# One output piece of a Fourier mixer in other tiles, and a new order of the kernel's front

## The chip, the cores and the metric

The kernel runs on one core of one Trainium2 chip. The metric is the time of one execution on the device in microseconds (us). Several executions were timed; their median is given, and one more was recorded by the hardware profiler.

## The reference

Two layers act on x, a sequence of 512 tokens of width 1024, under a conditioning vector c. Each has a token mixer and then a SwiGLU feed-forward network of width 2816. The mixer of layer 0 is a Fourier mixer, that of layer 1 a retention of 4 heads.

```python
c_act = jax.nn.silu(c)
...
mod = c_act @ w_ada[i] + b_ada[i]
sh1, sc1, g1, sh2, sc2, g2 = jnp.split(mod, 6, axis=-1)
h = modulate(rmsnorm(x, norm_mix_g[i]), sh1, sc1)
...
f = jnp.fft.fftn(hg, axes=(1, 3), norm="ortho").real.astype(h.dtype)
return f.reshape(B, S, D) @ w_o
...
x = x + g1[:, None, :] * m
h = modulate(rmsnorm(x, norm_ffn_g[i]), sh2, sc2)
x = x + g2[:, None, :] * swiglu(h, w_ffn_in[i], w_ffn_out[i])
```

`hg` is h in 4 groups of 256 channels, `w_o` is w_fourier_out. `modulate(h, shift, scale)` is `h * (1 + scale) + shift`; the six vectors of `mod` are named here (0,0) to (0,5) for layer 0: shift, scale and gate of the mixer, then shift (0,3), scale (0,4) and gate (0,5) of the feed-forward network.

## The kernel before, in words

**Products.** Every float32 matrix product is made of three products of rounded parts: high·high, high·low, low·high (`mm3`, L210 to L212). A weight piece of 128x1024 comes by DMA from the SP queue into a buffer `raw` (a pool of 8, so that a load waits until a buffer's last reader is done); `split` makes its high part on ACT (a cast, L204) and its low part on DVE (raw minus high, L205). The parts go into pools `highs` and `lows` of 5 buffers each, or, where the dict `homes` names a step, into two of the 14 held tiles `a0` to `a13` that are idle then (`high_low`, L310 to L324). For the four pieces of w_fourier_out that make the second half of the output channels, `by_dma` takes another way: ACT writes low = -raw (L319), GpSimd (POOL) starts an accumulating DMA that adds the piece from HBM (L321), and ACT casts the high part (L322).

**Conditioning.** A row block of w_ada is multiplied by c_act on DVE and summed (`conditioning`, L399, 128x1024); 8 such pieces, 0 to 7, make one vector of `mod`, and L411 and L414 close it with bias and gain. `settle(key, q)` runs the steps up to piece q.

**The front** (`front`, L654 to L792). It loads x in 4 row blocks, the sequence table in two pieces (into a12 and a13) and w_ada pieces. `squares`, `operand` and `table` make the rounded parts; `sums(m, n)` are the 12 sequence-transform products of block m for half n of the channels; `turn(m)` transposes block m of x on PE and copies it on ACT; `scaled(g)` writes channel group g, scaled by (0,1), to a tile (ACT, L737); `sines_of(g)` makes sine products (L744). In here `InOrder` fixes the order of ACT's and of PE's instructions as written.

**The Fourier output.** `sums_of_two(g)` and `lows_of_two(g)` make the cosine products of group g (L801), combine them with the sines on DVE (L808, L809), and make the two parts (cast L812, low L815). `out_product` then multiplies by w_fourier_out for the first 512 channels, and `out_product_last` for the others, in 256-token halves. Each result is added to x with gate (0,2) by `add_gated` (DVE, L579); its squares are summed over transposes of x on PE (L434); when a half's squares are complete, 1/rms is spread over partitions by two transposes (L459). Then the normed x is modulated (DVE L482, ACT L486 and L487), its low parts are made, and blocks are added and subtracted for a Strassen-like scheme (L516).

**The first feed-forward units** (`first_unit`). Unit 0 is plain (`PlainUnit`, L934), and unit 1 follows with `following.ps("12")` (L888). The pieces of their weights are here called by the buffer numbers of their parts: high/low 1142/1143, 1148/1149, 1154/1155 and 1160/1161 belong to unit 0, 1166/1167 and 1217/1218 to unit 1.

Outside `InOrder` the framework's scheduler sets each engine's order when the program is built. DVE, ACT, POOL and SP then work through their lists as they stand.

Of the kernel before, what the change touches and what calls it, by code (L numbers as in the profile page):

```python
# [156 lines left out]
def trunk(ctx, tc, A, where, out):  # L157
# [16 lines left out]
    def ps():  # L174
        return psum.tile([P, 512], F32, name="ps")
# [7 lines left out]
    def held(tag, dtype=F32R):  # L183

        return hpool.tile([P, D], dtype, name=tag)

    def tok(m):
        return slice(m * P, (m + 1) * P)

    def half(n):  # L190
        return slice(n * 512, (n + 1) * 512)
# [4 lines left out]
    def k2(t):  # L196
        return t.rearrange("p (k c) -> p k c", k=2)
# [453 lines left out]
    def fourier():  # L651
# [3 lines left out]
        def front():  # L655
# [26 lines left out]
            ch = [both[:, 3 * p * P : 3 * (p + 1) * P] for p in range(2)]  # L682
            issue(12)

            def turn(m):
                for k in range(2):
                    o = ps()
                    for j in range(4):
                        nc.tensor.transpose(o[:, tok(j)], xin[m][:, tok(4 * k + j)], ident)
                    for i in range(2):  # L690
                        src, dst = k2(o[:, part(i)]), k2(x[2 * k + i])
                        if m < 2:
                            nc.scalar.copy(out=dst[:, :, tok(m)], in_=src)
                        elif m == 2:
                            nc.scalar.copy(out=dst[:, :, hs : hs + 1], in_=src[:, :, 0:1])
                            nc.scalar.copy(out=dst[:, :, S - P + 1 : S], in_=src[:, :, P - 1 : 0 : -1])
                        else:
                            nc.scalar.copy(out=dst[:, :, hs + 1 : hs + 1 + P], in_=src[:, :, ::-1])
# [3 lines left out]
            def table(p):  # L702
                tabs.append((held(f"a{2 * p}"), held(f"a{2 * p + 1}")))
                split(*tabs[p], tab[p])
# [26 lines left out]
                    nc.tensor.matmul(banks[d], v[:, tok(d)], t[:, c], start=m == k == 0, stop=m == 3 and k == 2)  # L731

            def scaled(g):
                t = k2(held(f"a{g}", F32))
                for k in range(2):
                    d = 2 * g + k
                    nc.scalar.mul(out=t[:, k, :], in_=banks[d], mul=mods[0, 1][:, d : d + 1])  # L737
                a.append(t)
# [14 lines left out]
            with InOrder(tc, mybir.EngineType.Activation, mybir.EngineType.PE):  # L753
                nc.vector.tensor_scalar(out=gains, in0=gains, scalar1=1.0 / RS, scalar2=None, op0=ALU.mult)
                scales = bias[:, 0 : len(SCALES) * ND]
                nc.vector.tensor_scalar(out=scales, in0=scales, scalar1=1.0, scalar2=None, op0=ALU.add)
                squares(0)
                table(0)
                operand(0)
                sums(0, 0)  # L760
                squares(2)
                for n, c in enumerate(cs):
                    nc.scalar.activation(out=c_act[:, half(n)], in_=c, func=AF.Silu)
                squares(1)
                operand(2)
                settle((0, 1), 0)
                table(1)
                operand(1)
                turn(0)
                sums(2, 0)  # L770
                squares(3)
                operand(3)
                settle((0, 1), 3)
                turn(2)
                sums(1, 0)
                turn(1)
                sums(3, 0)
                settle((0, 1), 7)
                sums(0, 1)
                scaled(0)  # L780
                scaled(1)
                sums(2, 1)
                sines_of(0)
                sums(1, 1)
                settle((0, 0), 1)
                turn(3)
                sums(3, 1)
                scaled(2)
                scaled(3)
                sines_of(2)  # L790
            made.update(ch=ch, a=a, sines=sines)

        def halves_of(g):

# [48 lines left out]
        add(lambda: ordered(front))  # L843
        names = [[("wo", n, g) for g in range(4)] for n in range(2)]
        by_dma.update(names[1])
        for g in range(2):
            add(lambda g=g: ordered(lows_of_two, g))
            add(lambda g=g: ordered(sums_of_two, g))
        add(lambda: ordered(lows_of_two, 2))

        def between(g):
# [90 lines left out]
    def first_unit(u, following, channels=False):  # L942


        spread = lambda t, k: add(lambda: made["norm"].spread(t, k))
        if channels:
            homes[*u.key, "00", 0] = 4, 11
            add(last_sums)
            u.p(0, 0, 0)
            spread(0, 1)  # L950
            u.p(0, 0, 1)
            add(lambda: made["norm"].rate(1))
            spread(1, 0)
            u.p(0, 1, 0)
            spread(1, 1)
            u.p(0, 1, 1)
        else:
            homes[*u.key, "00", 0] = 3, 10
            homes[*u.key, "01", 0] = 5, 12
            u.p(0, 0, 0)  # L960
            add(last_sums)
            u.p(0, 0, 1)
            u.p(0, 1, 0)
            add(lambda: made["norm"].scale(1))
            u.p(0, 1, 1)
        following.ps("12")
        for k in range(2):
            for n in range(2):
                u.p(1, k, n)
# [379 lines left out]
```

## Time and profile before

| | |
|---|---|
| median of 3 executions | 1231.36 us (1231.19 to 1231.99) |
| profiled execution | 1231.14 us |
| its span in the trace | 1229.3 us |
| TensorE (PE) busy | 1203.0 us, 98% |
| VectorE (DVE) busy | 1042.1 us, 85% |
| ScalarE (ACT) busy | 583.5 us, 47% |
| GpSimd (POOL) busy | 4.5 us |
| mean granted clock of TensorE | 0.996 |

Busy is the time in which an engine had an instruction of its own in work. The sum over the span does not tell which engine sets the time of a stage; that is read from the stage's waits. The execution's time is 1.84 us more than its span.

### The profile page before, as it was taken

What the parts mean: (1) busy time and instruction counts of PE and PEld (TensorE: products, weight loads), DVE (VectorE), ACT (ScalarE), POOL (GpSimd) and SP (SyncE); (2) the same over time, 40 slices, a digit from 0 to 9 for tenths busy, and PEclk for the clock granted to TensorE, in tenths of its full rate; (3) what the DMA queues carried; (4) which work ended last, traced back from release to release, by engine and by line L of the source; (5) the groups of instructions that cost most, each with busy time, mean ns of one, the idle gap of its engine ahead of it and who ended that gap; (6) DMA issues with size and microseconds to landing.
All of it is one profiled execution on the core that took longest, in us unless ns stands there. A gap on an engine that the chain in (4) does not pass through costs nothing.

```text
span 1229.3 us, 20956 instructions
## 1 busy us (share of the span) xinstructions
PE 1203.0 (98%) x8456; PEld 1129.0 (92%) x8456; DVE 1042.1 (85%) x1702; ACT 583.5 (47%) x890; POOL 4.5 (0%) x12
## 2 busy tenths in 40 slices
PE   7999999999999999999999999999999999999996
PEld 6789998999999899999999999889999898989986
DVE  7989999889899669999898999956997787878755
ACT  5617653434345356455453554522765243434524
POOL 0000000000000000000000000000000000000000
PEclk9999999999999999999999999999999999999998
DMA  9994257464636522224243247852035243434302
GB/s 364 342 330 178 87 184 261 165 213 140 220 120 213 198 104 67 73 87 131 74 141 110 73 150 245 312 182 84 18 120 187 91 153 120 156 119 155 120 1 69
DMA packets 59872, 189.26 MB, mean 154 GB/s; under 512 B 6016, under 2 KB 14336, under 8 KB 59776
## 3 DMA queue, kind: packets, MB, share of 16 engines
q1 hardware_dynamic: 59200, 185.83, 44.3%
q0 software_dynamic: 576, 2.10, 0.9%
q8 instruction: 66, 1.08, 0.4%
q14 instruction: 30, 0.25, 0.1%
HBM read 180.57 MB, written 7.34 MB: 153 GB/s over the span
## 4 chain that ended last, share of the span: by engine, by line
PE 83%; DVE 8%; ACT 4%; DMA 2%; issue 2%; POOL 0%; SPq 0%; ACTq 0%; POOLq 0%; DVEq 0%
PE ps L888 46%; PE ps L211 11%; PE ps L210 11%; PE ps L212 11%; DVE low L205 2%; PE ps L934 2%; DVE raw L347 1%; PE ps L731 1%; ACT t4k L487 1%; PE ps L434 1%; DMA high<-in_w_ada 1%; DMA t4k<-in_x 1%; DMA low<-in_w_fourier_out 1%; ACT a L486 1%; ACT high L204 1%
## 5 line engine op out<-in xcount | busy, mean ns | idle before, releaser
L204 ACT CAST high<-raw 128x1024 fp32r<-128x1024 f32 x255 | 266.2, 1050 | 272.1 <-PE ps L888 80.0
L888 PE MATMUL ps<-a,high 128*128 128x256 f32 x2736 | 365.5, 283 | 2.2 <-ACT a L204 1.3
L205 DVE TENSOR_TENSOR low<-raw,high 128x1024 fp32r<-128x1024 f32 x255 | 310.4, 1221 | 64.0 <-ACT high L204 62.9
L888 PEld LDWEIGHTS ps<-a,high 128*128 128x128 f32 x2736 | 345.7, 192 | 4.7 <-ACT a L204 1.5
L888 PE MATMUL ps<-a,low 128*128 128x256 f32 x1368 | 192.1, 283 | 0.0
L210 PE MATMUL ps<-t4k,high 128*128 128x512 f32 (+1 forms) x512 | 182.2, 356 | 0.0
L211 PE MATMUL ps<-t4k,high 128*128 128x512 f32 (+1 forms) x512 | 179.0, 350 | 0.0
L212 PE MATMUL ps<-t4k,low 128*128 128x512 f32 (+1 forms) x512 | 178.7, 349 | 0.0
L888 PEld LDWEIGHTS ps<-a,low 128*128 128x128 f32 x1368 | 176.4, 192 | 0.1
L399 DVE SCALAR_TENSOR_TENSOR raw<-raw,c_act 128x1024 f32<-128x1024 f32 x97 | 117.7, 1221 | 26.6 <-DMA raw<-in_w_ada 17.3
L212 PEld LDWEIGHTS ps<-t4k,low 128*128 128x128 f32 x512 | 96.6, 189 | 12.6
L888 PE MATMUL ps<-high,a 128*128 128x256 f32 x784 | 107.0, 283 | 1.0 <-ACT t2k L897 0.7
L579 DVE SCALAR_TENSOR_TENSOR x<-ps,mod,x 128x512 f32<-128x512 f32 (+1 forms) x132 | 81.0, 634 | 31.6 <-PE ps L212 31.3
L210 PEld LDWEIGHTS ps<-t4k,high 128*128 128x128 f32 x512 | 96.7, 189 | 11.9
L211 PEld LDWEIGHTS ps<-t4k,high 128*128 128x128 f32 x512 | 96.9, 189 | 11.7
L897 ACT COPY t2k<-ps 128x512 f32<-128x512 f32 x96 | 56.2, 586 | 98.0 <-PE ps L888 95.2
L888 PEld LDWEIGHTS ps<-high,a 128*128 128x128 f32 x784 | 100.4, 192 | 2.5 <-ACT t2k L897 0.9
L901 DVE TENSOR_TENSOR t2k<-t2k,ps 128x512 f32<-128x512 f32 x96 | 65.5, 683 | 13.7 <-ACT t2k L897 8.7
L347 DVE TENSOR_TENSOR raw<-raw 128x1024 f32<-128x1024 f32 x62 | 75.6, 1219 | 0.2
L212 PE MATMUL ps<-a,low 128*128 128x512 f32 (+1 forms) x160 | 56.2, 352 | 2.8 <-DMA low<-in_w_fourier_out 2.8
L204 ACT CAST t4k<-t2k 128x512 fp32r<-128x512 f32 x73 | 45.0, 619 | 29.1 <-DVE t2k L1007 20.8
L210 PE MATMUL ps<-a,high 128*128 128x512 f32 (+1 forms) x160 | 56.9, 359 | 0.2 <-ACT t2k L807 0.2
(157 smaller groups left out, 1428.7 us busy)
## 6 DMA issues: line engine op xcount, KB each, us to landing
raw<-in_w_ffn_in SPq DMA_DIRECT2D x86, 512.0 KB, 4.1
raw<-in_w_ada SPq DMA_DIRECT2D x81, 512.0 KB, 4.5
raw<-in_w_ret_in SPq DMA_DIRECT2D x48, 512.0 KB, 3.3
raw<-in_w_ffn_out SPq DMA_DIRECT2D x44, 512.0 KB, 3.9
raw<-in_w_ret_out SPq DMA_DIRECT2D x16, 512.0 KB, 4.9
raw<-in_w_ada_final SPq DMA_DIRECT2D x16, 512.0 KB, 3.5
raw<-in_w_fourier_out SPq DMA_DIRECT2D x8, 512.0 KB, 7.9
t4k<-in_w_ada SPq DMA_DIRECT2D x7, 512.0 KB, 9.5
```

What stands on the lines that cost most here:

```text
L204: nc.scalar.copy(out=dst_h, in_=src)
L205: nc.vector.tensor_tensor(out=dst_l, in0=src, in1=f32(dst_h), op=ALU.subtract)
L210: nc.tensor.matmul(o, ah, bh, start=first, stop=False, **kw)
L211: nc.tensor.matmul(o, ah, bl, start=False, stop=False, **kw)
L212: nc.tensor.matmul(o, al, bh, start=False, stop=last, **kw)
L347: eng.tensor_tensor(out=dst, in0=p, in1=q, op=ALU.subtract)
L399: nc.vector.scalar_tensor_tensor(out=t, in0=t, scalar=1.0, in1=c_act, op0=ALU.mult, op1=ALU.mult, accum_out=v[:, q : q + 1])
L579: nc.vector.scalar_tensor_tensor(out=xt(j)[:, sl], in0=o, scalar=mods[key][:, j : j + 1], in1=xt(j)[:, sl], op0=ALU.mult, op1=ALU.add)
L888: nc.tensor.matmul(o[:, j * 256 : (j + 1) * 256], a, b, start=tag in "127" and n == m == j == k == 0, stop=n == 1 and k == 3, skip_group_c ...
L897: nc.scalar.copy(out=t, in_=o)
L901: nc.vector.tensor_tensor(out=t, in0=t, in1=self.z if tag == "5" else o, op=ALU.add)
L934: nc.tensor.matmul(o[:, j * 256 : (j + 1) * 256], a, b, start=k == n == m == j == c == 0, stop=k == n == 1 and c == 3, skip_group_check=True,)
```

## The change

Four things are done. (1) The last piece of w_fourier_out, ("wo", 1, 3), gets the held tiles a4 and a11 for its parts; the first piece of the first feed-forward unit, which had these, goes to the pools. (2) `scaled(g)` writes to a12, a13, a2 and a3, where the raw and the split tables were, and no longer to a0 to a3. (3) `turn` is split into `turn` (PE) and `keep` (ACT), and the front is written in another order: SiLU of c first, x turned sooner. (4) `sines_of(2)` stands behind `sums_of_two(0)`, so cosine products of group 0 come first.

```diff
-            def turn(m):
-                for k in range(2):
-                    o = ps()
+            turned = {}
+            def turn(m):
+                turned[m] = [ps() for _ in range(2)]
+                for k, o in enumerate(turned[m]):
                     for j in range(4):
                         nc.tensor.transpose(o[:, tok(j)], xin[m][:, tok(4 * k + j)], ident)
+            def keep(m):
+                for k, o in enumerate(turned.pop(m)):
                     for i in range(2):
...
-                t = k2(held(f"a{g}", F32))
+                t = k2(held(f"a{(12, 13, 2, 3)[g]}", F32))
...
+                for n, c in enumerate(cs):
+                    nc.scalar.activation(out=c_act[:, half(n)], in_=c, func=AF.Silu)
+                cs.clear()
                 squares(0)
+                turn(0)
                 table(0)
                 operand(0)
                 sums(0, 0)
                 squares(2)
-                for n, c in enumerate(cs):
-                    nc.scalar.activation(out=c_act[:, half(n)], in_=c, func=AF.Silu)
                 squares(1)
+                turn(2)
                 operand(2)
-                settle((0, 1), 0)
                 table(1)
                 operand(1)
-                turn(0)
+                squares(3)
+                keep(0)
                 sums(2, 0)
-                squares(3)
+                turn(1)
+                settle((0, 1), 0)
                 operand(3)
+                keep(2)
+                sums(1, 0)
                 settle((0, 1), 3)
-                turn(2)
-                sums(1, 0)
-                turn(1)
+                keep(1)
+                turn(3)
                 sums(3, 0)
+                keep(3)
...
-                turn(3)
                 sums(3, 1)
                 scaled(2)
                 scaled(3)
-                sines_of(2)
...
-        for g in range(2):
-            add(lambda g=g: ordered(lows_of_two, g))
-            add(lambda g=g: ordered(sums_of_two, g))
+        homes["wo", 1, 3] = 4, 11
+        add(lambda: ordered(sums_of_two, 0))
+        add(lambda: ordered(made["sines_of"], 2))
+        add(lambda: ordered(sums_of_two, 1))
         add(lambda: ordered(lows_of_two, 2))
...
-            homes[*u.key, "00", 0] = 4, 11
```

The order in which the instructions stand changes at places that the diff does not name. The first is DVE's list at the end of the w_fourier_out products. mod2 is the gate (0,2), mod4 and mod3 are the scale (0,4) and the shift (0,3), ps are banks of products. Before:

```order
L399 SCALAR_TENSOR_TENSOR raw_595,mod4_1022<-raw_595,c_act_88 128x1024
L399 SCALAR_TENSOR_TENSOR raw_589,mod2_705<-raw_589,c_act_88 128x1024
L399 SCALAR_TENSOR_TENSOR raw_602,mod4_1022<-raw_602,c_act_88 128x1024
L399 SCALAR_TENSOR_TENSOR raw_655,mod4_1022<-raw_655,c_act_88 128x1024
L411 TENSOR_TENSOR mod2_705<-mod2_705,vectors_89 128x8
L399 SCALAR_TENSOR_TENSOR raw_696,mod4_1022<-raw_696,c_act_88 128x1024
L579 SCALAR_TENSOR_TENSOR x0_92<-ps_540,mod2_705,x0_92 128x512
L579 SCALAR_TENSOR_TENSOR x0_92<-ps_541,mod2_705,x0_92 128x512
L579 SCALAR_TENSOR_TENSOR x1_93<-ps_542,mod2_705,x1_93 128x512
L579 SCALAR_TENSOR_TENSOR x1_93<-ps_543,mod2_705,x1_93 128x512
L579 SCALAR_TENSOR_TENSOR x2_94<-ps_757,mod2_705,x2_94 128x256
L411 TENSOR_TENSOR mod4_1022<-mod4_1022,vectors_89 128x4
```

With the change:

```order
L399 SCALAR_TENSOR_TENSOR raw_655,mod4_1022<-raw_655,c_act_88 128x1024
L399 SCALAR_TENSOR_TENSOR raw_696,mod4_1022<-raw_696,c_act_88 128x1024
L399 SCALAR_TENSOR_TENSOR raw_703,mod3_1037<-raw_703,c_act_88 128x1024
L411 TENSOR_TENSOR mod4_1022<-mod4_1022,vectors_89 128x4
L399 SCALAR_TENSOR_TENSOR raw_589,mod2_705<-raw_589,c_act_88 128x1024
L414 TENSOR_TENSOR mod4_1022<-mod4_1022,vectors_89 128x4
L399 SCALAR_TENSOR_TENSOR raw_707,mod3_1037<-raw_707,c_act_88 128x1024
L399 SCALAR_TENSOR_TENSOR raw_710,mod3_1037<-raw_710,c_act_88 128x1024
L399 SCALAR_TENSOR_TENSOR raw_713,mod3_1037<-raw_713,c_act_88 128x1024
L411 TENSOR_TENSOR mod2_705<-mod2_705,vectors_89 128x8
L411 TENSOR_TENSOR mod3_1037<-mod3_1037,vectors_89 128x4
L579 SCALAR_TENSOR_TENSOR x0_92<-ps_540,mod2_705,x0_92 128x512
```

The additions to x (L579) now stand behind four conditioning pieces of (0,3), and the last piece of the gate, raw_589, behind the first of these. The buffer of raw_589 is the one into which raw_713 is loaded.

The second place is DVE's list at unit 0 of the feed-forward network, behind the spread of the second half's 1/rms (ps_1247). Before:

```order
L205 TENSOR_TENSOR low_1161<-raw_1045,high_1160 128x1024
L232 SCALAR_TENSOR_TENSOR rs_y1_1113<-rs_u1_1115,rs_y1_1113 128x1
L205 TENSOR_TENSOR low_1167<-raw_1140,high_1166 128x1024
L482 SCALAR_TENSOR_TENSOR t4k_1250<-x0_92,mod4_1022,ps_1247 128x256 x2
L482 SCALAR_TENSOR_TENSOR t4k_1250<-x1_93,mod4_1022,ps_1247 128x256 x2
L205 TENSOR_TENSOR low_1218<-raw_1146,high_1217 128x1024
L516 TENSOR_TENSOR t4k_1252<-t4k_1250,t4k_1251 128x512
L482 SCALAR_TENSOR_TENSOR t4k_1303<-x2_94,mod4_1022,ps_1247 128x256 x2
```

With the change, two fences that follow one another:

```order
L482 SCALAR_TENSOR_TENSOR t4k_1250<-x0_92,mod4_1022,ps_1247 128x256 x2
L482 SCALAR_TENSOR_TENSOR t4k_1250<-x1_93,mod4_1022,ps_1247 128x256 x2
L205 TENSOR_TENSOR low_1161<-raw_1045,high_1160 128x1024
L516 TENSOR_TENSOR t4k_1252<-t4k_1250,t4k_1251 128x512
L482 SCALAR_TENSOR_TENSOR t4k_1303<-x2_94,mod4_1022,ps_1247 128x256 x2
L516 TENSOR_TENSOR t4k_1252<-t4k_1250,t4k_1251 128x512
L482 SCALAR_TENSOR_TENSOR t4k_1303<-x3_95,mod4_1022,ps_1247 128x256 x2
L516 TENSOR_TENSOR a13_1305<-t4k_1303,a6_1304 128x512
L516 TENSOR_TENSOR t4k_1049<-t4k_1049,t4k_1250 128x512 x2
L516 TENSOR_TENSOR a13_1305<-t4k_1303,a6_1304 128x512
L516 TENSOR_TENSOR a11_1321<-t4k_1049,a4_1320 128x512 x2
L516 TENSOR_TENSOR t4k_1049<-t4k_1303,t4k_1049 128x512 x2
```

```order
L516 TENSOR_TENSOR t4k_1250<-t4k_1250,t4k_1303 128x1024
L205 TENSOR_TENSOR a9_1329<-t4k_1049,a2_1328 128x512 x2
L205 TENSOR_TENSOR a12_1338<-t4k_1250,a5_1337 128x1024
L516 TENSOR_TENSOR t4k_1196<-t4k_1196,t4k_1049 128x1024
L205 TENSOR_TENSOR low_1167<-raw_1140,high_1166 128x1024
L1016 TENSOR_TENSOR t2k_1301<-ps_1222,t2k_1301 128x512
L205 TENSOR_TENSOR a10_1343<-t4k_1196,a3_1342 128x1024
L347 TENSOR_TENSOR raw_1140<-raw_1152,raw_1140 128x1024
L205 TENSOR_TENSOR t4k_1375<-t2k_1301,t4k_1374 128x2x256
L347 TENSOR_TENSOR t2_1269<-raw_1158,raw_1140 128x1024
L347 TENSOR_TENSOR raw_1152<-raw_1158,raw_1152 128x1024
L205 TENSOR_TENSOR low_1218<-raw_1146,high_1217 128x1024
```

low_1167 and low_1218, the first two low parts of unit 1, stood ahead of the modulation's L516 work and now stand behind nearly all of it.

The third place is PE's list at the same stage, with the change: both L459 stand together; this is the second, and what stands behind it.

```order
L459 MATMUL ps_1247<-ident_96,rs_y1_1113 128x128
L944 MATMUL ps_1170<-a1_1197,high_1154 128x256 x8
L944 MATMUL ps_1170<-a1_1197,low_1155 128x256 x8
L944 MATMUL ps_1170<-a8_1198,high_1154 128x256 x8
L944 MATMUL ps_1222<-a1_1197,high_1160 128x256 x8
L944 MATMUL ps_1222<-a1_1197,low_1161 128x256 x8
L944 MATMUL ps_1222<-a8_1198,high_1160 128x256 x8
L898 MATMUL ps_1383<-a0_1050,high_1166 128x256 x8
L898 MATMUL ps_1383<-a0_1050,low_1167 128x256 x8
L898 MATMUL ps_1383<-a7_1051,high_1166 128x256 x8
L898 MATMUL ps_1416<-a1_1197,high_1217 128x256 x8
L944 MATMUL ps_1443<-t4k_1251,high_1142 128x256 x8
```

In this list 56 matmuls stand between the second L459 and the eight that read low_1167, and 32 more, these eight among them, before those that read low_1218, which stand right behind the last row; in the kernel before, the products stood in the same order but for the first L459 and for one group of eight.

On POOL, whose list holds the four transfers of L321, the one of ("wo", 1, 3) moves from the fourth place to the second, and ACT's L319 and L322 for it move ahead of those of ("wo", 1, 1) and ("wo", 1, 2).

## Rows read from the trace of the kernel before

**Rows 1.** Page, parts 1 and 4: TensorE's busy time; engines' shares of the chain.

```profile
PE 1203.0 (98%) x8456; PEld 1129.0 (92%) x8456; DVE 1042.1 (85%) x1702; ACT 583.5 (47%) x890; POOL 4.5 (0%) x12
...
PE 83%; DVE 8%; ACT 4%; DMA 2%; issue 2%; POOL 0%; SPq 0%; ACTq 0%; POOLq 0%; DVEq 0%
```

**Rows 2.** Timeline of PE, 74 to 84 us (start, duration, what, [idle before <-releaser]).

```profile
75.02 0.28 PE L211 MATMUL ps<-a,high 128*128 128x256 f32 x1
78.06 0.39 PE L212 MATMUL ps<-a,low 128*128 128x256 f32 x1 [2.75 <-DMA low<-in_w_fourier_out]
...
78.64 0.82 PE L434 MATMUL ps<-ident,x 128*128 128x128 f32 x6
```

**Rows 3.** Windows: stretch, length, busy PE, PEld, DVE, ACT, POOL, granted clock, DMA share, GB/s.

```profile
79.40:82.80 3.40, 3.40 (x18) 3.40 (x17) 3.40 (x6) 0.00 (x0) 0.00 (x0) 0.50 1.02 405
50.00:80.00 30.00, 27.25 (x136) 23.28 (x135) 26.69 (x53) 10.88 (x17) 3.59 (x4) 0.99 1.04 344
```

**Rows 4.** Timeline of POOL, 46 to 80 us.

```profile
53.14 1.00 POOL L321 DMA_DIRECT2D low<-in_w_fourier_out  x1 [8.21 <-DVE low L205]
...
69.59 0.86 POOL L321 DMA_DIRECT2D low<-in_w_fourier_out  x1 [6.32 <-ACT low L319]
```

**Rows 5.** Transfers issued at 69.2 to 69.6 us: KB each, median us to landing.

```profile
raw<-in_w_ada SPq DMA_DIRECT2D x2, 512.0 KB, 9.4
low<-in_w_fourier_out POOLq DMA_DIRECT2D x1, 512.0 KB, 8.4
```

**Rows 6.** Transfers issued at 55 to 55.5 us.

```profile
raw<-in_w_ada SPq DMA_DIRECT2D x1, 512.0 KB, 17.5
```

**Rows 7.** Transfers issued at 62 to 62.3 us.

```profile
raw<-in_w_ada SPq DMA_DIRECT2D x1, 512.0 KB, 12.1
```

**Rows 8.** Transfers issued at 107 to 110 us.

```profile
raw<-in_w_ffn_in SPq DMA_DIRECT2D x2, 512.0 KB, 3.3
```

**Rows 9.** Timeline of DVE, 72 to 80 us.

```profile
72.28 1.22 DVE L399 SCALAR_TENSOR_TENSOR raw<-raw,c_act 128x1024 f32<-128x1024 f32 x1
...
73.43 2.72 DVE L579 SCALAR_TENSOR_TENSOR x<-ps,mod,x 128x512 f32<-128x512 f32 x4
78.83 0.48 DVE L579 SCALAR_TENSOR_TENSOR x<-ps,mod,x 128x256 f32<-128x256 f32 x1 [2.69 <-PE ps L212]
```

**Rows 10.** Timeline of PE, 30 to 48 us.

```profile
32.04 2.43 PE L744 MATMUL ps<-a,t4k 128*128 128x256 f32 x8 [0.83 <-ACT a L737]
```

**Rows 11.** Chain of waits, 105 to 140 us (start, duration, what).

```profile
112.86 0.11 PE ps L459
112.97 3.95 PE ps L934 x33
116.92 5.76 PE ps L888 x48
```

**Rows 12.** Timeline of DVE, 109 to 126 us.

```profile
112.51 1.22 DVE L205 TENSOR_TENSOR low<-raw,high 128x1024 fp32r<-128x1024 f32 x1
113.64 1.65 DVE L482 SCALAR_TENSOR_TENSOR t4k<-x,mod,ps 128x256 f32<-128x256 f32 x4
115.21 1.22 DVE L205 TENSOR_TENSOR low<-raw,high 128x1024 fp32r<-128x1024 f32 x1
116.36 0.69 DVE L516 TENSOR_TENSOR t4k<-t4k 128x512 fp32r<-128x512 f32 x1
116.97 0.86 DVE L482 SCALAR_TENSOR_TENSOR t4k<-x,mod,ps 128x256 f32<-128x256 f32 x2
...
121.98 1.22 DVE L516 TENSOR_TENSOR t4k<-t4k 128x1024 f32<-128x1024 f32 x1
123.11 0.68 DVE L901 TENSOR_TENSOR t2k<-t2k,ps 128x512 f32<-128x512 f32 x1
```

**Rows 13.** Windows of the rest of the program, same columns.

```profile
135.00:400.00 265.00, 264.09 (x1896) 250.19 (x1895) 241.70 (x298) 121.38 (x149) 0.00 (x0) 1.00 0.55 187
400.00:700.00 300.00, 298.45 (x2203) 284.56 (x2202) 262.08 (x490) 149.90 (x230) 0.00 (x0) 1.00 0.32 106
700.00:1000.00 300.00, 298.32 (x2039) 277.47 (x2038) 250.63 (x403) 143.38 (x218) 0.00 (x0) 1.00 0.45 151
1000.00:1229.30 229.30, 219.43 (x1571) 207.18 (x1569) 168.87 (x244) 95.24 (x142) 0.00 (x0) 0.99 0.34 111
```

More of the change, by code (lines that the diff above doesn't have):

```diff
@@ L789, in front @@
                 scaled(3)
-                sines_of(2)
-            made.update(ch=ch, a=a, sines=sines)
+            made.update(ch=ch, a=a, sines=sines, sines_of=sines_of)
         def halves_of(g):
```

## Prediction

> **What bounds the kernel now.** First the page: TensorE (PE) is busy 1203.0 of 1229.3 us and carries 83% of the chain that ended last [rows 1]. A time can only change by PE idling more or less, or by its clock. So I looked for PE's idle stretches near the change, then for what other engines finish just ahead of PE there.
>
> PE's timeline shows one large stretch: its matmul at 75.02 is followed by one at 78.06, which waited for the low part of a w_fourier_out piece [rows 2]. That part is written by POOL's fourth transfer, issued at 69.59 and landing 8.4 us later, at 78.0 [rows 4, 5]. A matmul of 256 columns follows the one before it by 0.12 us here, so about 2.9 us are lost. Behind the stall the granted clock is 0.50 (1.2 GHz) from 79.40 to 82.80 [rows 3]: 18 matmuls take 3.4 us where 18 x 0.12 = 2.2 would do, so 1.2 us more go there. The stall is worth 2.9 + 1.2 = 4.1 us.
>
> At the first feed-forward unit the chain of waits is PE itself: 33 products of unit 0 in 3.95 us and 48 of unit 1 in 5.76, each 0.12, with nothing between them [rows 11]. DVE is just as full: between 112.51 and 123.11 each instruction starts about when the one before ends [rows 12]. So an instruction moved forward or back in DVE's list there moves in time by the cost of what it passes.
>
> **The change, part by part.** *Tiles for the last piece, transfer second in line.* Its transfer is issued some 15 us sooner (first at 53.14, last at 69.59 now [rows 4]), so even at the longest landing shown, 17.5 us [rows 6], it is there before 75. The wait for it goes.
>
> *What is late next: the additions to x.* PE's next work is L434, at 78.64 [rows 2], which transposes the updated x. Now DVE runs L579 from 73.43, before the stall ends [rows 9], so nothing more is asked of it. In the new list L579 stands behind raw_703, raw_589, raw_707, raw_710 and raw_713, and raw_713 can be loaded only when raw_589's buffer is free. raw_703 was issued at 55.2 and took 17.5 us [rows 6], landing at 72.8; raw_707 took 12.1 from 62.1 and landed at 74.2 [rows 7]; raw_710 and raw_713, issued near 69.3, took 9.4 in the median [rows 5] and so landed near 78.7, beside POOL's last transfer. Walk: raw_703 multiplied from 72.8 to 74.0, raw_589 (1.15 more) to 75.1, then raw_713 is issued. It lands 3.3 later if nothing stands in its way [rows 8], at 78.4; its multiplication ends at 79.6, two small L411 add 0.2, and three L579 of 2.72 / 4 = 0.68 each [rows 9] end at 81.8. That is 3.2 later than L434 starts now.
>
> Two things shift this walk. The fourth POOL transfer now lies ahead of raw_703, not behind it. With the DMA engines full (share 1.04 at 344 GB/s from 50 to 80 us [rows 3]), 0.524 MB take 1.5 us: later by 1.5. Bounds: nothing, and 3.3, one whole unhindered load [rows 8]. The Trainium skill ("DMA: Bandwidth & Descriptors", Anatomy of one DMA, SWDGE path) fits such a transfer by 2.0 us plus bytes over 436 GB/s, an estimate of 3.2 us; the row has 8.4 for the last one. By the page this piece would have been there at 72.8 and PE would not have waited for it at all; the measurement decides, and the queue was not empty. Against the 1.5 stands what the front gains: PE now waits 0.83 us for a scaled group before L744 [rows 10], and a second time as long at 41.67. The new tiles hold nothing that sums still read, and cosines come first, so both waits can go: 1.7 sooner, and the loads that wait for buffers which PE frees move along. Net 0.2 sooner; the x update ends 3.0 late. The half-clock stretch stays, since PE idles some 6 us instead of 3. **Term A: +3.0.** Bounds: -4.1 (the stall goes, nothing replaces it) and +4.9 (no front gain, transfer at 1.5 plus 0.2).
>
> The rest of the front (SiLU first, x turned sooner, casts that stand behind more ACT work) I cost at nothing: what releases L434 is then a load and DVE, which don't wait for it. If that cover were gone, it is bounded by the 1.7 above, inside A's bounds.
>
> *The first feed-forward unit.* PE reaches the eight products that read low_1167 56 matmuls behind the second L459: 56 x 0.12 = 6.7 us. DVE starts its list for that half about 0.4 us after L459 (between 0 and the 0.67 from 112.97 to 113.64 [rows 11, 12]). From starts of consecutive rows [rows 12]: four L482 take 1.57, a low part of 1024 columns 1.14, an L516 or other 512-column step 0.61; the 1024-column L516 runs from 121.98 to 123.11, 1.13. Ahead of low_1167 stand eight L482 (3.15), low_1161 (1.14), ten L516 of 512 (6.1), two low parts of 512 (1.2) and three 1024-column steps (3.4): 15.0. With 0.4 before and 1.22 of its own, low_1167 is ready 16.6 us after L459. PE waits 16.6 - 6.7 = 9.9. **Term B: +9.9.** ACT's parts between L482 and L516 could only delay it. Below: DVE's list can't be shortened by a faster predecessor, as both sides count from the same L459; above: a half-clock stretch behind so long an idle time, 1.2 as after the first stall [rows 3].
>
> Behind low_1167, DVE has two 512 steps (1.2), four of 1024 (4.5) and low_1218 (1.2): 7.0 us. PE has 32 matmuls: 3.84. So it waits again, 3.2. **Term C: +3.2.** If PE runs at half clock, its 32 matmuls take 6.8 and the wait is 0.2: the same sum. So C covers the clock's loss in that case, and 1.2 stays as a bound above.
>
> *Given back.* DVE has done its backlog while PE stood, so PE's idle 0.91 from 135 to 400 us [rows 13] may vanish. **Term D: -0.9**, between -0.9 and 0. The dropped calls of lows_of_two(0) and (1) did nothing; the homes entry moves a piece to the pools at the same price for its two parts.
>
> Sum: 3.0 + 9.9 + 3.2 - 0.9 = +15.2. Against the profiled execution's 1231.1 that is **1246.3 us** (the median of the runs, 1231.4, differs by 0.2). Bounds: -4.1 + 9.9 + 3.2 - 0.9 = +8.1, or 1239.2; and 4.9 + 9.9 + 3.2 + 1.2 = +19.2, or 1250.3.
>
> **Rivals.** *1. The stall's gain comes through.* If raw_703 and raw_713 land sooner by as much as the walk is late, L434 starts when the products end: A = -4.1, sum +8.1, 1239.2 us. For it: raw loads wait for buffers that the front frees, and the front is shorter. Against it: the DMA engines are full from 50 to 80 us [rows 3], and raw_713's chain alone, 75.1 + 3.3 + 1.2 + 0.2 + 2.0, leaves the loads no slack.
>
> *2. Not slower: PE's idle time later in the program takes the delay in.* PE idles 0.9 + 1.6 + 1.7 + 9.9 = 14.0 us behind 135 us [rows 13]. If these waits are for loads and for DVE's backlog, which run on while PE stands, they shrink by what PE is late: 15.2 - 14.0 = +1.2, 1232.3 us. It decides if the 9.9 at the end is such a wait. Against it: these last 229 us have a DMA share of 0.34 and DVE 74% busy [rows 13]; idle there looks like a chain at the end that starts when PE is done, and without it only 4.1 can be taken in.
>
> *3. The change does only what it says.* DVE's list is written, but if low_1167 has other work of PE's behind which it hides, B and C go: A - 0.9, at best -5.0, 1226 us. PE's list has 56 matmuls there and no more, so this needs PE to be slowed elsewhere.
>
> **How the numbers follow.** The forecast, with its bounds above rival 1, has 0.66; rival 1 0.22; rival 2 0.07; rival 3 0.05. A measurement of this kernel can tell about 0.2%, 2.5 us, from no change. Rival 2 lies within it: same 0.07. Rival 3 is faster: 0.05. The rest is slower: 0.88. The range goes from below rival 1 (1237, for another 2 us of front) to 1251; it leaves out rivals 2 and 3 and a little at both ends.
>
> **What would show it.** In the new profile PE's idle time before L212 of the last piece is gone, and its wait before L434 at about 75 to 82 us is released by DVE's L579, behind an L399 that waited for a load. A second idle stretch of some 10 us stands before products of unit 1 (now L898), released by DVE's L205, with a shorter one soon after. Wrong would be: L579 done before 78.6; PE full from its second L459 to 135 us; or an end of the program at which less idle time is left than 9.9.

## The result, and the profile after

The changed kernel takes **1245.41 us** (median of 4 runs, 1244.51 to 1246.13), the kernel before 1231.35 in the same comparison (4 runs). The ratio is 1.0114, with a 95% interval of 1.0102 to 1.0126: slower by 14.1 us. The forecast was 1246.3 us, with a range of 1237 to 1251. The profiled execution of the changed kernel took 1245.00 us, with a span of 1243.0, so 13.7 us more of span than before.

The waits of PE tell most of it. This is the list of PE's waits over the whole program, for the changed kernel (who waited, for whom, us in total, times, longest):

```profile
PE ps L898 <- DVE low L205: 9.8, 1, 9.8
PE ps L434 <- DVE x L579: 3.2, 2, 3.0
...
PE ps L210 <- ACT a L821: 2.7, 1, 2.7
...
PE ps L898 <- ACT high L204: 2.0, 2, 1.6
...
PE ps L810 <- DVE a L838: 1.2, 1, 1.2
```

The wait for the w_fourier_out piece (2.75 in [rows 2]) is no longer in the list. In its place stand 9.8 us in which unit 1's products wait for a low part, 3.0 in which L434 waits for the additions to x, and two waits in the front that were not there before.

Page of the changed kernel, parts 1 and 4, against [rows 1]: PE is busy about as long, and DMA and DVE hold a larger part of the chain together.

```profile
PE 1204.7 (97%) x8456; PEld 1130.4 (91%) x8456; DVE 1042.7 (84%) x1702; ACT 584.4 (47%) x890; POOL 4.5 (0%) x12
...
PE 83%; DVE 7%; DMA 5%; ACT 4%; issue 1%; SPq 0%; ACTq 0%; DVEq 0%
```

Timeline of PE, changed kernel, at the three places (start, duration, what, [idle before <-releaser]):

```profile
47.69 1.69 PE L210 MATMUL ps<-a,high 128*128 128x512 f32 x4 [2.67 <-ACT a L821]
...
77.39 0.28 PE L212 MATMUL ps<-a,a 128*128 128x256 f32 x1
80.68 0.44 PE L434 MATMUL ps<-ident,x 128*128 128x128 f32 x2 [3.00 <-DVE x L579]
...
111.33 0.38 PE L459 MATMUL ps<-ident,rs_y 128*128 128x128 f32 x2
...
117.29 1.12 PE L898 MATMUL ps<-a,high 128*128 128x256 f32 x8
128.18 2.08 PE L898 MATMUL ps<-a,low 128*128 128x256 f32 x8 [9.77 <-DVE low L205]
...
133.58 2.07 PE L898 MATMUL ps<-a,high 128*128 128x256 f32 x8 [1.62 <-ACT high L204]
...
137.07 1.12 PE L898 MATMUL ps<-a,low 128*128 128x256 f32 x8
```

The first output product stands at 47.69. The last w_fourier_out product of the first token half starts at 77.39 and waits for nothing, where in the kernel before the last four stood behind the wait that ended at 78.06 [rows 2]; L434 then waits until 80.68, where it stood at 78.64. The two L459 of the second half start at 111.33, and the products that read low_1167 at 128.18, 9.77 us after PE had run out of work: seven groups of eight had stood between, and the last of them is done at 118.4.

Windows of the changed kernel, same columns as [rows 3]:

```profile
47.60:52.00 4.40, 4.31 (x12) 3.41 (x13) 4.33 (x10) 3.50 (x6) 0.86 (x1) 0.61 1.01 349
80.70:84.00 3.30, 3.30 (x28) 3.30 (x29) 3.30 (x5) 0.00 (x0) 0.00 (x0) 1.00 1.03 411
118.00:128.00 10.00, 0.41 (x4) 0.20 (x2) 10.00 (x14) 5.79 (x10) 0.00 (x0) 0.76 0.00 0
128.00:133.00 5.00, 3.79 (x16) 3.49 (x16) 5.00 (x7) 1.70 (x4) 0.00 (x0) 0.50 0.00 0
1000.00:1243.00 243.00, 233.14 (x1685) 220.89 (x1683) 181.37 (x258) 101.08 (x149) 0.00 (x0) 0.99 0.34 111
```

The granted clock is 0.50 (1.2 GHz) behind the long wait (128 to 133) and 0.61 in the mean at 47.6 to 52, but 1.00 (2.4 GHz) behind the wait before L434. The last 229 us of before with 9.87 of idle time [rows 13] are the last 243 here with 9.86: nothing was taken in there.

How far the changed kernel is behind the kernel before, at points of the program that both traces have:

| point | before | changed | behind |
|---|---|---|---|
| first output product (L210) | 47.35 | 47.69 | 0.34 |
| first L434 | 78.64 | 80.68 | 2.04 |
| first L459 | 100.20 | 100.79 | 0.59 |
| first product with low_1167 | 117.72 | 128.18 | 10.46 |
| third ACT copy of unit products (L897, now L907) | 143.02 | 158.39 | 15.37 |
| ninth such copy | 184.91 | 198.71 | 13.80 |
| thirtieth | 402.37 | 416.17 | 13.80 |

From the ninth copy to the thirtieth, all 22 rows say 13.80 within 0.14.

### The profile page after: what moved, and what is told of

It reads as the page before. It is cut to its first block, busy times and chain, and to the rows that moved or that the text cites. A ratio compares the mean times of both kernels' runs of the same rounds, so it can differ in the third digit from the quotient of the medians.

```text
span 1243.0 us, 20972 instructions
## 1 busy us (share of the span) xinstructions
PE 1204.7 (97%) x8456; PEld 1130.4 (91%) x8456; DVE 1042.7 (84%) x1702; ACT 584.4 (47%) x890; POOL 4.5 (0%) x12
## 4 chain that ended last, share of the span: by engine, by line
PE 83%; DVE 7%; DMA 5%; ACT 4%; issue 1%; SPq 0%; ACTq 0%; DVEq 0%
PE ps L898 48%; PE ps L210 11%; PE ps L211 11%; PE ps L212 11%; DMA raw<-in_w_ada 3%; DVE low L205 1%; ACT t4k L487 1%; PE ps L944 1%; DVE t4k L516 1%; ACT a L486 1%; DMA high<-in_w_ada 1%; DMA t4k<-in_w_ada 1%; PE ps L434 1%; DVE raw L399 1%; DVE raw L347 1%
## 5 line engine op out<-in xcount | busy, mean ns | idle before, releaser
L898 PE MATMUL ps<-a,high 128*128 128x256 f32 x2736 | 366.7, 284 | 2.9 <-ACT high L204 1.6
L898 PEld LDWEIGHTS ps<-a,high 128*128 128x128 f32 x2736 | 347.1, 193 | 5.2 <-ACT high L204 1.9
L898 PE MATMUL ps<-a,low 128*128 128x256 f32 x1368 | 193.0, 284 | 9.8 <-DVE low L205 9.8
L898 PEld LDWEIGHTS ps<-a,low 128*128 128x128 f32 x1368 | 177.2, 193 | 10.0 <-DVE low L205 10.0
L210 PE MATMUL ps<-t4k,high 128*128 128x512 f32 (+1 forms) x512 | 182.2, 356 | 0.0
L212 PEld LDWEIGHTS ps<-t4k,low 128*128 128x128 f32 x512 | 96.6, 189 | 12.7
L898 PE MATMUL ps<-high,a 128*128 128x256 f32 x784 | 107.0, 283 | 1.0 <-ACT t2k L907 0.7
L210 PEld LDWEIGHTS ps<-t4k,high 128*128 128x128 f32 x512 | 96.7, 189 | 11.9
L579 DVE SCALAR_TENSOR_TENSOR x<-ps,mod,x 128x512 f32<-128x512 f32 (+1 forms) x132 | 80.8, 634 | 29.9 <-PE ps L212 29.6
L907 ACT COPY t2k<-ps 128x512 f32<-128x512 f32 x96 | 56.2, 585 | 102.7 <-PE ps L898 99.8
L898 PEld LDWEIGHTS ps<-high,a 128*128 128x128 f32 x784 | 100.4, 192 | 2.5 <-ACT t2k L907 0.9
L347 DVE TENSOR_TENSOR raw<-raw 128x1024 f32<-128x1024 f32 x62 | 75.6, 1219 | 0.3
L205 DVE TENSOR_TENSOR t4k<-t2k,t4k 128x512 fp32r<-128x512 f32 x73 | 49.9, 685 | 7.0 <-ACT t4k L204 7.0
L898 PE MATMUL ps<-low,a 128*128 128x256 f32 x392 | 55.4, 283 | 0.0
```

The source lines that it names most:

```text
L205: nc.vector.tensor_tensor(out=dst_l, in0=src, in1=f32(dst_h), op=ALU.subtract)
L210: nc.tensor.matmul(o, ah, bh, start=first, stop=False, **kw)
L212: nc.tensor.matmul(o, al, bh, start=False, stop=last, **kw)
L347: eng.tensor_tensor(out=dst, in0=p, in1=q, op=ALU.subtract)
L579: nc.vector.scalar_tensor_tensor(out=xt(j)[:, sl], in0=o, scalar=mods[key][:, j : j + 1], in1=xt(j)[:, sl], op0=ALU.mult, op1=ALU.add)
L898: nc.tensor.matmul(o[:, j * 256 : (j + 1) * 256], a, b, start=tag in "127" and n == m == j == k == 0, stop=n == 1 and k == 3, skip_group_c ...
```

## The experiments

Each run was timed beside the kernel before; the medians of before were 1231.3 in all of them.

### Part (1) alone: e1_homes_only

On the kernel before:

```diff
         by_dma.update(names[1])
+        homes["wo", 1, 3] = 4, 11
...
-            homes[*u.key, "00", 0] = 4, 11
```

> The kernel before with part (1) of the change alone: the last piece of w_fourier_out in a4 and a11, unit 0's first piece in the pools; the front as before. Theory (DVE's and PE's order at the unit sets the price): low_1167 stands ahead of the L482 here, so no wait for it; low_1218 stands behind 15.0 us of DVE work from the second L459, ready at 16.6, while PE has some 99 matmuls, 11.9 us, before it: a wait of about 4.7 us, followed by half clock at 1 to 2. The stall of 2.9 + 1.2 at 75 us goes. Time about 1231.4 - 4.1 + 4.7 + 1 = 1233, range 1231 to 1235. Rival (the unit's loss comes from unit 0's first piece being in the pools, whatever the order): the loss of 14 to 15 us of the unit is here in full, 1241 or more. Rival (all loss comes from the front): 1227.

Measured: 1231.59 us (10 runs), ratio 1.0005 (0.9996 to 1.0015). L434 starts at 75.66, 2.98 sooner than before; the stall at 75 us is gone. But PE waits 3.83 us at the unit, and for another tile than expected:

```profile
115.14 1.12 PE L889 MATMUL ps<-a,high 128*128 128x256 f32 x8
120.09 1.21 PE L889 MATMUL ps<-a,high 128*128 128x256 f32 x8 [3.83 <-ACT high L204]
```
```profile
117.49 1.12 ACT L558 CAST a<-t4k 128x512 fp32r<-128x512 f32 x2
118.52 0.57 ACT L898 COPY t2k<-ps 128x512 f32<-128x512 f32 x1
119.00 1.04 ACT L204 CAST high<-raw 128x1024 fp32r<-128x1024 f32 x1
```

(Timelines of PE and of ACT.) The wait is for the cast of high_1217, not for low_1218. In ACT's list this cast stands behind the modulation's work and the copy of unit 1's first products (L898 here). With unit 0's first piece in the pool, the parts of five pieces fill its five buffers, and high_1217 is the sixth. The time came out as the theory has it, and the rivals' 1241 and 1227 did not, but low_1218 was the wrong tile.

### The new front alone: e2_front_only

On the changed kernel:

```diff
-        homes["wo", 1, 3] = 4, 11
...
         if channels:
+            homes[*u.key, "00", 0] = 4, 11
```

> The changed kernel without part (1): unit 0's first piece in a4 and a11 again, the last piece of w_fourier_out in the pools; the new front stays. Theory: low_1167 stands behind 9.1 us of DVE work from the second L459, ready at 10.7, and PE has 75 matmuls, 9.0 us, before it: a wait of about 1.7; low_1218 follows at once, no wait of its own. L434 still waits for the additions behind (0,3), at 80 to 82 us, so about +1 at the first L459. Time 1231.4 + 0.6 + 1.7 + 1 = 1234, range 1232 to 1237. Rival (the front's order delays everything that follows): 1243 or more. Rival (pools): 1232.

Measured: 1234.79 us (9 runs), ratio 1.0024 (1.0014 to 1.0034). The time is near the 1234 expected, but it is made otherwise:

```profile
80.99 0.58 PE L212 MATMUL ps<-a,low 128*128 128x256 f32 x1 [3.94 <-DMA low<-in_w_fourier_out]
...
123.31 1.22 PE L897 MATMUL ps<-a,high 128*128 128x256 f32 x8 [1.61 <-ACT high L204]
```

(Timeline of PE.) The piece's transfer is again the fourth, issued at 71.33, later than the 69.59 of [rows 4], and PE waits 3.94 us for it; L434 comes at 82.01, behind that, so the additions to x were covered. low_1167 cost no wait; the cast of high_1217 cost 1.61. ACT runs that cast at 122.23, with no wait of its own, right behind the last L487 of the modulation. So the new front alone brings no gain here; the old stall is longer under it.

### Unit 1's parts sooner: e3_unit_early

On the changed kernel, a priority for the split of unit 1's pieces (`early` holds the key of the unit that follows):

```diff
-            ready[step] = combined(step)
+            with tc.high_priority(offset=4 * URGENT if step[:3] in early else 0):
+                ready[step] = combined(step)
```

> The changed kernel with one thing more: the parts of unit 1's pieces get a higher priority, so that DVE has low_1167 right behind low_1161 and low_1218 in the middle of the L482, as in the kernel before. Nothing else is undone. Theory: the 9.8 us wait for low_1167, and the 5.05 us of wait and half clock behind it, go; what the program gave back afterwards (1.8) goes too: 1245.4 - 14.9 + 1.8 = 1232.3, range 1231 to 1235 (the L516 are later by three L347 and a low part, which may cost 1 to 3). Rival (the unit's weights come late, by loads or pools): no change, 1244 or more.

Measured: 1232.69 us (10 runs), ratio 1.0007 (0.9997 to 1.0016), 12.7 us less than the changed kernel. PE's waits now:

```profile
PE ps L436 <- DVE x L581: 3.9, 2, 3.6
...
PE ps L900 <- ACT high L204: 1.5, 2, 1.1
```

The 9.8 for the low part is gone, of the cast's wait 1.1 is left at the unit, and L436 (L434, moved by two lines) waits as before. The priority moves the low parts in DVE's list and the casts in ACT's. So the places of unit 1's parts in these lists are what cost the 9.8 and most of the 5 behind it; the loads of the same pieces were in time. Where this 1.1 comes from, ACT's timeline shows:

```profile
122.34 1.04 ACT L204 CAST high<-raw 128x1024 fp32r<-128x1024 f32 x1 [4.05 <-PE ps L900]
```

ACT stood 4.05 us before the cast of high_1217, until PE had done the last eight products that read high_1166 (121.18 to 122.30). The cast reads nothing that PE makes, so it waited for a buffer: here the shortage itself is seen.

### The additions to x sooner: e4_x_first

On the changed kernel, a priority for the gate's conditioning and for its closing in `settle`:

```diff
-            conditioning(step, loads.pop(step))
+            with tc.high_priority(offset=8 * URGENT if step[1:3] == (0, 2) else 0):
+                conditioning(step, loads.pop(step))
...
-                for _ in it:
-                    pass
+                with tc.high_priority(offset=8 * URGENT if key == (0, 2) else 0):
+                    for _ in it:
+                        pass
```

> The changed kernel with a higher priority for the conditioning pieces of the gate (0,2) and its closing, so that DVE's additions to x stand ahead of the four (0,3) pieces, as in the kernel before. Theory: PE's wait of 3.0 us before L434 (77.5 to 80.7) goes; the stall at the unit stays: 1245.4 - 3.2 = 1242.2, range 1241 to 1243.5. If a half-clock stretch comes with it, less. Rival (L434 waits for the loads whatever stands in DVE's list, or the (0,3) pieces are late at L486 then): no change, 1245 or more.

Measured: 1242.00 us (4 runs), ratio 1.0089 (1.0074 to 1.0104): 3.4 less than the changed kernel. L434 follows the last product at once (77.50 behind 77.38), and the wait at the unit stays:

```profile
PE ps L900 <- DVE low L205: 10.0, 1, 10.0
```

### The piece in other idle tiles: e5_homes_1_8 and e6_after_1_8

If the shortage of buffers for six pieces sets where unit 1's parts stand, another pair of idle tiles for the w_fourier_out piece should keep the gain and not the loss. e5 is the kernel before with one line:

```diff
         by_dma.update(names[1])
+        homes["wo", 1, 3] = 1, 8
```

> The kernel before with its last piece of w_fourier_out in a1 and a8, two other held tiles that are idle then; unit 0's first piece keeps a4 and a11, and the front is as before. So of the change only the earlier transfer is left. In DVE's and ACT's lists low_1167 stands behind the first four L482 as before, and the cast of high_1217 ahead of the modulation's L486. Theory (the stall at 75 us is worth 2.9 + 1.2, the unit's loss comes from where unit 1's parts stand, which this does not touch): 1231.3 - 4.1 = 1227.2, up to 1229 if DVE's own lag at 166 to 185 us takes back what PE gains. Rival (the stall at 75 us is hidden behind DVE or loads anyway): 1231.

Measured: 1227.43 us (6 runs), ratio 0.9969 (0.9956 to 0.9981). The first L434 stands at 75.82, the waits at the unit are gone, and from the second ACT copy on the kernel is 3.38 us ahead of the one before.

e6 is the changed kernel with the same tiles:

```diff
-        homes["wo", 1, 3] = 4, 11
+        homes["wo", 1, 3] = 1, 8
...
         if channels:
+            homes[*u.key, "00", 0] = 4, 11
```

> The changed kernel, but the last piece of w_fourier_out lies in a1 and a8, and unit 0's first piece in a4 and a11 again; all else stays. Theory: with six pieces' parts wanted in pools of five, the cast of high_1217 waited for the buffer of high_1166, and the scheduler put unit 1's low parts late; with the tile pair given back both come early without any priority, so the waits of 9.8 and 1.6 at the unit go, while the 3.0 before L434 stays: 1245.4 - 14.9 + 1.8 - 1.1 = 1231.2, range 1230 to 1233. Rival (the new front, not the tiles, makes the unit's loss): 1243 or more.

Measured: 1230.19 us (10 runs), ratio 0.9996 (0.9987 to 1.0005): 15.2 less than the changed kernel, by a choice of tiles alone. PE's waits:

```profile
PE ps L434 <- DVE x L579: 2.7, 2, 2.5
PE ps L210 <- ACT a L821: 2.7, 1, 2.7
```

None for a low part or for the cast of high_1217 is left.

### Both repairs, and a later sine: e7 to e9

e7 is e6 with e4's priority.

> As the run before it, and the conditioning of the gate (0,2) with the higher priority, so that the additions to x stand ahead of (0,3). Theory: the 3.0 to 3.6 before L434 go as well, 1231.2 - 3.4 = 1227.8, range 1226.5 to 1229.5; about as far as the kernel before with the tiles a1 and a8 alone. Rival (the two waits hide one another): no gain against the run before it.

Measured: 1227.22 us (5 runs), ratio 0.9969 (0.9956 to 0.9981), 3.0 less than e6. The two waits add up and don't hide one another.

In e7 PE still waits 1.16 and 2.67 us in the front. e8 tried to move that, with e3's priority kept in it:

```diff
-        add(lambda: ordered(made["sines_of"], 2))
         add(lambda: ordered(sums_of_two, 1))
+        add(lambda: ordered(made["sines_of"], 2))
```

> As the run before it, with sines_of(2) one place later, behind sums_of_two(1), and unit 1's parts with the higher priority too. In DVE's list group 0's combinations then stand ahead of the low parts of three w_fourier_out pieces, and in ACT's its casts ahead of the copy of the sines. Theory (in the changed kernel PE idled 1.2 and 2.7 us at 41 to 48 us because group 0's DVE and ACT work stood behind that, and ran at half clock until 52): the products start at 44 to 45 us, 2 to 4 us sooner: 1227.8 - 3 = 1224.8, range 1223 to 1228. Rival (behind 50 us the loads of the gate's pieces bound the additions to x): no gain, 1228, and a wait before L434 of 2 to 4.

Measured: 1234.39 us (6 runs), ratio 1.0028 (1.0016 to 1.0039): 7 us worse than e7, a plain miss. The trace shows where: at the unit, PE waits twice for an L516 (L520 here), and DVE's timeline says why.

```profile
PE ps L948 <- DVE a L520: 3.9, 2, 2.8
```
```profile
103.42 4.62 DVE L205 TENSOR_TENSOR low<-raw,high 128x1024 fp32r<-128x1024 f32 x4
107.97 1.22 DVE L350 TENSOR_TENSOR raw<-raw 128x1024 f32<-128x1024 f32 x1
109.10 0.68 DVE L520 TENSOR_TENSOR a<-t4k,a 128x512 fp32r<-128x512 f32 x1
109.70 1.22 DVE L350 TENSOR_TENSOR t<-raw 128x1024 f32<-128x1024 f32 x1
110.84 1.22 DVE L350 TENSOR_TENSOR raw<-raw 128x1024 f32<-128x1024 f32 x1
111.97 1.22 DVE L350 TENSOR_TENSOR raw<-raw,t 128x1024 f32<-128x1024 f32 x1
113.11 0.68 DVE L520 TENSOR_TENSOR a<-t4k,a 128x512 fp32r<-128x512 f32 x1
```

Four low parts, 4.62 us, and an L350 stand ahead of the first L520, and three more L350, 3.4 us, between it and the second, for which PE waits longest. L350 (L347 before) prepares raw pieces of unit 1. With the tiles given back, the pieces are ready early, and the priority put unit 1's ahead of the modulation that PE needs first. So the same priority that gave 12.7 us in e3 costs here.

e9 is e8 without that priority.

> The run e8 without the higher priority for unit 1's parts, so against e7 only sines_of(2) one place later. Theory: e8 lost at the unit, where the priority put the low parts of unit 0 and 1 ahead of the modulation's first steps (PE waited 2.8 for an L516 there, and 1.1 more); without it the loss of 7 us against e7 goes: 1227 to 1229. At the front e8 gained nothing over e7 at L434 (78.98 against 78.73), so neither will this: no better than 1226.5. Rival (the later sines themselves cost the 7 us): 1233 or more.

Measured: 1228.38 us (11 runs), ratio 0.9978 (0.9969 to 0.9987). Of the 7 us 6.0 are back, by the priority alone, so they were the priority's. The later sine itself gives nothing: PE now waits 2.67 for a scaled group's first column (L840), and 1.7 for a piece's transfer.

```profile
PE ps L812 <- DVE a L840: 2.7, 1, 2.7
...
PE ps L212 <- DMA low<-in_w_fourier_out: 1.7, 1, 1.7
```

### Part (2) on e5: e10_1_8_scaled

```diff
-                t = k2(held(f"a{g}", F32))
+                t = k2(held(f"a{(12, 13, 2, 3)[g]}", F32))
```

> The run e5 (the kernel before with the last piece in a1 and a8) with part (2) of the change as well: scaled groups in a12, a13, a2 and a3; no new order. Theory: the two waits of 0.83 before the sine products go, PE is up to 1.7 us ahead at the first output product, and since the products up to L434 run without a wait there, it keeps most of it: 1227.4 - 1.2 = 1226.2, range 1225.5 to 1227.4. Rival (the 0.83 returns as a longer wait for group 0's casts, as in the changed kernel): 1227.4 or more.

Measured: 1226.78 us (5 runs), ratio 0.9962 (0.9950 to 0.9975): the lowest median of all, though its 0.65 less than e5 is within what these runs can tell apart. One of the two waits before L744 is left (0.78), the first output product starts at 45.19 and the first L434 at 74.23, against 47.30 and 75.82 in e5.

## Why the prediction was right, point by point

**The sum held: +15.2 was forecast, +14.1 was measured**, or 13.9 between the two profiled executions. The bound that it named, DVE's list at the first units, is the bound; e3 and e6 each remove some 13 to 15 us there. That the sum is off by 1.1 only is in part luck: term A came out 2.4 short of its 3.0 and term C 1.9 over its 3.2, and the two nearly cancel. No part makes the loss alone: the tiles by themselves cost 0.3 us net (e1) and the front 3.5 (e2), so about 10 of the 14 come only where the two meet. With the tiles alone low_1167 stands early in DVE's list, and with the front alone PE's list has more work ahead of it; the scheduler's list with both has neither.

**Term B, +9.9: measured 9.77.** DVE begins its list 0.41 us behind the start of the two L459 (0.4 was taken), and the eight L482, the L516 and the rest follow. DVE's timeline of the changed kernel, where the list begins and ends, and 6 us later:

```profile
111.74 1.66 DVE L482 SCALAR_TENSOR_TENSOR t4k<-x,mod,ps 128x256 f32<-128x256 f32 x4 [0.28 <-PE ps L459]
...
125.76 1.22 DVE L516 TENSOR_TENSOR t4k<-t4k 128x1024 f32<-128x1024 f32 x1
126.90 1.22 DVE L205 TENSOR_TENSOR low<-raw,high 128x1024 fp32r<-128x1024 f32 x1
...
133.78 1.22 DVE L205 TENSOR_TENSOR low<-raw,high 128x1024 fp32r<-128x1024 f32 x1
```

low_1167 runs from 126.90 to 128.12, 16.8 us behind L459's 111.33, where 16.6 were reckoned. PE's next product starts at 128.18.

**Term C, +3.2: measured 5.05, and by another cause.** The step that failed is "So it waits again, 3.2", for low_1218. PE came to the products of low_1218 at 137.07, and low_1218, the last row above, was done at 135.0. What PE waited for was high_1217, 1.62 us, whose cast stands on ACT behind a copy (L907) of the products that PE had just made (ACT's timeline):

```profile
132.00 0.58 ACT L907 COPY t2k<-ps 128x512 f32<-128x512 f32 x1 [2.61 <-PE ps L898]
132.48 1.05 ACT L204 CAST high<-raw 128x1024 fp32r<-128x1024 f32 x1
```

The other 3.4 us are the clock at 0.50: the 32 matmuls from 128.18 on take 8.9 us with the wait, where 3.84 were due. "C covers the clock's loss" was wrong too, since the cast is behind PE's own products, and so moves with the clock. At full clock and with the cast in time PE would have come to low_1218 at 132.0 and waited 3.0, an estimate from 128.18 plus 3.84 and the 135.0: the wait that was forecast lay hidden behind the two others. A term was missing as well: the prediction said of the homes entry that it "moves a piece to the pools at the same price", and did not look for a buffer that would be short. e3 shows the shortage as a wait of ACT; e1 (3.83 us for the cast), e3 (1.1) and e6 (nothing) price it. That the cast's late place in the changed kernel's list comes from the shortage alone is not shown: in e2, with unit 0's first piece in its tiles again, the cast cost 1.61 too, from its place behind the modulation.

**Term A, +3.0: +2.04 at L434, and +0.59 at the first L459.** The right wait took the stall's place: PE stood 3.0 us for L579, and e4 gave 3.4 back by DVE's order alone. The walk, with its two shifts, put the first L579 at 79.6, and it came at 79.87, but by another way: that is luck. Three steps were off. First, "raw_713 can be loaded only when raw_589's buffer is free", which the section on the change says too: raw_713, the third load issued after raw_703, was issued at 67.6 us and took 9.9, and raw_589 was read until 76.2. So it had another buffer. DVE's timeline of the changed kernel:

```profile
73.71 1.22 DVE L399 SCALAR_TENSOR_TENSOR raw<-raw,c_act 128x1024 f32<-128x1024 f32 x1 [0.38 <-DMA raw<-in_w_ada]
...
74.94 1.22 DVE L399 SCALAR_TENSOR_TENSOR raw<-raw,c_act 128x1024 f32<-128x1024 f32 x1
...
76.16 1.21 DVE L399 SCALAR_TENSOR_TENSOR raw<-raw,c_act 128x1024 f32<-128x1024 f32 x1
...
77.30 1.22 DVE L399 SCALAR_TENSOR_TENSOR raw<-raw,c_act 128x1024 f32<-128x1024 f32 x1
...
78.45 1.22 DVE L399 SCALAR_TENSOR_TENSOR raw<-raw,c_act 128x1024 f32<-128x1024 f32 x1
...
79.87 3.12 DVE L579 SCALAR_TENSOR_TENSOR x<-ps,mod,x 128x512 f32<-128x512 f32 x5
```

The five multiplications run back to back from 73.71, when raw_703 had landed, to 79.60. Behind that landing the wait is five times DVE's own 1.15 us, and not a chain of loads. raw_703 itself landed at 73.7, 0.9 later than the row of before had it, with its issue 1.3 us sooner. What the transfer costs such a load, e5 shows, where only the transfer moves: the load issued at 55.2 took 19.9 us, 2.4 more than in [rows 6], where 1.5 was reckoned. Second, "three L579 of 2.72 / 4 = 0.68 each": L434 started at 80.68, 0.81 behind the start of the first L579, so it waits for one of them and not for three. That 1.2 us less is why L434 came 1.0 us sooner than the forecast had it. Third, "The half-clock stretch stays": behind 3.0 us of idle time the clock was 1.00 from 80.7 to 84, so 1.2 of loss went, and that is most of the difference from 2.04 to 0.59.

The fit of the Trainium skill ("DMA: Bandwidth & Descriptors", Anatomy of one DMA, SWDGE path) gives an estimate of 3.2 us for a POOL transfer; the last one took 8.5 here, as far off as before.

**The front, reckoned as 1.7 us sooner: 0.3 later.** Both waits before the sine products went, and the last sequence sums ended 2.9 us sooner (37.97 against 40.85). But then PE waited 1.17 and 2.67 us, and ran at a mean clock of 0.61 up to 52. DVE's timeline shows what was late next:

```profile
42.39 3.49 DVE L205 TENSOR_TENSOR low<-raw,high 128x1024 fp32r<-128x1024 f32 x3
45.80 0.42 DVE L817 TENSOR_TENSOR t2k<-ps,t2k 128x256 f32<-128x256 f32 x1
```

The combinations of group 0 (L817), whose parts the first output product reads, stand behind three low parts of w_fourier_out pieces. The step that failed is "both waits can go: 1.7 sooner": the waits went, the gain did not follow. That the rest of the front costs nothing held in the changed kernel, where L434 waited for DVE in any case; it doesn't once that wait is taken away: L434 stands at 77.50 in e4, with the new front, and at 75.66 in e1, with the old one and the same tiles, so the new front is 1.8 us late there. Over the whole program nothing of it is left to see: e7 and e5, with the tiles a1 and a8 and the one front or the other, take 1227.2 and 1227.4. e9 moved the sines and won nothing, so which order of the front would help stays open.

**Term D, -0.9: -1.57**, between the seventh and the ninth copy of the table (15.37 to 13.80), at 166 to 185 us of before, where PE idled 0.9. This much of rival 2 is true, and no more. The reason given, that DVE works off its backlog while PE stands, does not hold: PE's waits there in the kernel before are for casts on ACT (0.69 us at 178.38, 0.22 at 179.81), and e7, where PE never stood at the unit, takes back the same 1.57 (1.77 us ahead of the kernel before at the seventh copy, 3.34 at the ninth), while e5 keeps the two waits and takes back nothing. Why they go, and what makes the other 0.7, stays open.

**Rivals.** Rival 1 (1239.2) asked the walk of term A to be covered; it was late by two thirds of what was said. Rival 2 fell with the last window above, and rival 3 with the 9.77.

## What to carry to other kernels

Where a scheduler sets an engine's list, a change of tiles can move instructions far from it. Print each engine's list before and after, and count what stands ahead of the instruction for which the matrix engine waits next: here the count was right to 0.2 us. An idle tile isn't free if another piece had been promised it: that piece goes to a pool, and the pool's last buffer may decide what can be made ahead; another pair of tiles gained 3.9 us on the kernel before (e5) where the first gained nothing (e1), and under the new front the two are 15.2 us apart (e6). And a priority that repairs one list can break the next (12.7 us gained in e3, 6.0 lost in e8 against e9), so that it should go where the shortage is, not on top.

## What the runs showed of the hardware that was not expected

Idle time alone doesn't say whether the clock falls. Behind 2.75 us of idle time the kernel before ran at 0.50 for 3.4 us [rows 2, 3]; behind 3.00 us at the same place, the changed kernel ran at 1.00. Both came to the wait from products that had run without one since 48 us. At that place e6 ran at 1.00 behind 2.49 us, and e3 at 0.50 behind 3.65. What made the difference no run here tells.
